# First attention's scores: two 128-row products per component replaced by three 64-row products, the two components side by side in the array's rows

## The chip, the cores and the metric

The kernel runs on one core of a Trainium2 chip. The metric is device time in microseconds (us) of one execution; less is better. Five engines work side by side on a core, each through its own queue in order: PE (TensorE, matrix products), DVE (VectorE), ACT (ScalarE), POOL (GpSimd) and SP (SyncE, which here only issues DMA transfers). A matrix product takes a stationary operand, which is loaded into PE's array first (rows "PEld" of the profile), and a moving operand that streams past it; the contraction runs over the partitions, and the result lands in a bank of PSUM, the accumulator memory, from where DVE or ACT must read it before the bank can be used again.

## The reference, cut to what matters

One decoder layer on a sequence of 1024 positions with model width 1024. Its first attention is a differential attention: 4 heads, each with two components of width 64, whose two softmaxes are subtracted. The other parts (a dilated window attention, gates, output projections, a gated feed-forward layer with a short convolution) are not touched by the change.

```python
def diff_attention(q, k, v, lam):        # q, k: (B, S, H, 2, 64), v: (B, S, H, 128)
    scale = dqk ** -0.5
    def one_block(args):                 # one block of 128 queries
        qi, i = args
        sc = jnp.einsum('bqhcd,bkhcd->bchqk', qi, k).astype(jnp.float32) * scale
        qpos = i * Q_BLOCK + jnp.arange(Q_BLOCK)
        causal = kpos[None, :] <= qpos[:, None]
        p = jax.nn.softmax(jnp.where(causal, sc, -jnp.inf), axis=-1)
        a = p[:, 0] - lam * p[:, 1]
        return jnp.einsum('bhqk,bkhd->bqhd', a, v)
```

Before this, q and k of a head are projections of the normed input, turned by rotary embedding. All of it is asked for in float32.

## The kernel before

**Precision.** PE works here on operands of a type called fp32r, and the kernel does not take one fp32r copy of a float32 operand as exact enough. So an operand is split into a high part (a copy to fp32r, done by ACT) and a low part (operand minus high part, done by DVE); the helper is `split`, whose two instructions show as L149 (ACT) and L146 (DVE). A product of two split operands is three PE products, high by high, low by high and high by low; the helper is `mm3`, lines L155, L156 and L157.

**Projection.** `proj_t` loads the weights of 128 columns, and for each half of the sequence (512 positions) makes 8 times `mm3` into one PSUM bank (the tile `acc`), 24 products of 512 columns. When the bank is full, an evacuation function is called. For the first attention, `proj_a(h)` does this for q and then for k of head h. The 128 rows of the result are the head's two components, 64 rows each. The evacuation first calls `rotated`: four ACT copies (L684) and three DVE instructions (L685 to L687), which leave the turned half in a tile `t`.

**How q and k are laid out.** The scores of one component have a contraction of 64, half of the array's rows. The kernel uses the other half for the low part. For component 0, tile `q0` holds the high part of q in rows 0 to 63 and its low part in rows 64 to 127; `k0` holds the high part of k in both halves of the rows, and `l0` the low part of k in both. Then q0 by k0 is high by high plus low by high, and q0 by l0 is high by low plus low by low. So a component takes two 128-row products, L765 and L766. (`q1`, `k1` and `l1` are the same for component 1.) This layout costs 64-row instructions: for a half of q two ACT copies (L730, L731) and two DVE subtractions (L732, L733), for a half of k four ACT copies (L738, L739, two each) and four DVE subtractions (L742). Every head takes six tiles from a ring of 18 (`slot`).

**Scores.** `attend_a(h, i)` handles one block of 128 queries, i from 0 to 7. It needs the scores against the first (i+1)*128 keys, cut into pieces of at most 512 columns: one piece for i up to 3, two for i from 4 to 7. For each component, and for each of its pieces, it takes a PSUM bank from a pool of two (tile `s` on PE, `ps_s` in the code), makes the two products, and has DVE add the mask, find the row's maximum and write the scores to SBUF (L768). Then ACT takes the exponential (L777), DVE combines the two components (L784), and the block's probabilities are later turned on PE (L697) and multiplied with v (L710, L713).

**Order of the work.** The program is written as one stream, and a scheduler at build time orders it for each engine: of the instructions whose operands and buffers it expects to be there, it takes the one that stands first in the stream, with the attention's pieces moved ahead by 30 places (`high_priority(offset=30)`). The blocks of a head come in the order i = 6, 7, 4, 5, 2, 3, 0, 1. Between them stand other pieces of work that only need PE and its operands (`interleave`, `A_FILLS`): the projections of the next head, gates, and for the last head the first projections of the dilated attention. So the products of a projection stand between the products of the scores on PE wherever a score product was not expected to be ready.

Of the kernel before, what the change touches and what calls it, by code (L numbers as in the profile page):

```python
# [15 lines left out]
F32 = mybir.dt.float32  # L16
F32R = mybir.dt.float32r
I32 = mybir.dt.int32
AF = mybir.ActivationFunctionType
ALU = mybir.AluOpType  # L20
# [4 lines left out]
P = 128  # L25
S = 1024
# [33 lines left out]
QA, KA, VA, QB, KB, VB, GT = 0, 512, 1024, 1536, 3072, 4608, 6144  # L60
# [27 lines left out]
def trunk(ctx: ExitStack, tc: tile.TileContext, a, out):  # L88
    nc = tc.nc
# [17 lines left out]
    def psum(dt=F32, pool=acc, tag="acc"):  # L107
        return pool.tile([P, 512], dt, tag=tag, name=tag)
# [39 lines left out]
    def split(hi, lo, src, eng=None):  # L148
        copy = nc.scalar.activation(hi, src, AF.Copy)  # L149
        sub(eng or nc.vector, lo, src, hi)  # L150
        return copy.ins
# [83 lines left out]
    def proj_t(col, evacuate):  # L235

        wh, wl = load_unit(w_in[where[col]])
        for half, sl in enumerate(halves()):
            ps = psum()
            for k in range(KC):  # L240
                w = slice(k * P, (k + 1) * P)
                mm3(ps, wh[:, w], wl[:, w], xh[:, k, sl], xl[:, k, sl], k == 0, k == KC - 1)
                if k == KC - 1:
                    evacuate(half, sl, ps)
                if k % 2:
                    yield 0.5
# [65 lines left out]
    ps_s = open_pool(attn, "ps_s", bufs=2, space=PSUM)  # L312
# [18 lines left out]
    def slot(name, shape=(P, S), dt=F32R):  # L331

        return slots.tile(list(shape), dt, tag="slot", name=name, bufs=SLOTS)
# [111 lines left out]
    with ExitStack() as st_y:  # L445
# [115 lines left out]
        with ExitStack() as st0:  # L561
# [18 lines left out]
            for j in range(KC):  # L580
# [7 lines left out]
                c = 0  # L588
# [27 lines left out]
        for n in range(8, len(steps_v)):  # L616
# [25 lines left out]
            if k == 0 and (p, i) in places_y:  # L642
                q, name, pool = places_y[p, i]
# [12 lines left out]
    cos_a, sin_a = load_tabs(64, 32)  # L656
# [22 lines left out]
    def rotated(ps, cos, sin, sl, quarter):  # L679
        t1 = rt.tile([P, 512], F32, tag="t1", name="t1")  # L680
        t2 = rt.tile([P, 512], F32, tag="t2", name="t2")
        for q in range(P // quarter):
            src, dst = slice((q ^ 1) * quarter, ((q ^ 1) + 1) * quarter), slice(q * quarter, (q + 1) * quarter)
            nc.scalar.activation(t1[dst], ps[src], AF.Copy)  # L684
        nc.vector.tensor_tensor(t2, ps, cos[:, sl], op=ALU.mult)  # L685
        nc.vector.tensor_tensor(t1, t1, sin[:, sl], op=ALU.mult)
        nc.vector.tensor_tensor(t2, t2, t1, op=ALU.add)  # L687
        return t2
# [28 lines left out]
    wk_a = open_pool(st_a, "work_a", side="right")  # L717
# [4 lines left out]
    u, v = slice(0, 64), slice(64, 128)  # L722

    def proj_a(h, res):
        q0, q1, k0, k1, l0, l1 = (slot(n) for n in ("q0", "q1", "k0", "k1", "l0", "l1"))
        res += [q0, q1, k0, k1, l0, l1]

        def put_q(half, sl, ps):
            t = rotated(ps, cos_a, sin_a, sl, 32)
            nc.scalar.activation(q0[u, sl], t[u], AF.Copy)  # L730
            nc.scalar.activation(q1[v, sl], t[v], AF.Copy)  # L731
            nc.vector.tensor_tensor(q0[v, sl], t[u], q0[u, sl].bitcast(F32), op=ALU.subtract)  # L732
            nc.vector.tensor_tensor(q1[u, sl], t[v], q1[v, sl].bitcast(F32), op=ALU.subtract)  # L733

        def put_k(half, sl, ps):
            t = rotated(ps, cos_a, sin_a, sl, 32)
            for part, kk in ((u, k0), (v, k1)):
                nc.scalar.activation(kk[u, sl], t[part], AF.Copy)  # L738
                nc.scalar.activation(kk[v, sl], t[part], AF.Copy)  # L739
            for part, kk, ll in ((u, k0, l0), (v, k1, l1)):  # L740
                for to in (u, v):
                    nc.vector.tensor_tensor(ll[to, sl], t[part], kk[part, sl].bitcast(F32), op=ALU.subtract)  # L742

        yield from proj_t(QA + h * P, put_q)
        yield from proj_t(KA + h * P, put_k)

    def attend_a(h, i, ops, vs, out_sb, pair):

        q0, q1, k0, k1, l0, l1 = ops
        scale = QK ** -0.5  # L750
        if i // 4 not in out_sb:
            out_sb[i // 4] = (wk_a.tile([P, 512], F32, tag="osb", name="osb", bufs=2),
                              tiny.tile([P, 4], F32, tag="eps4", name="eps4", bufs=2))
        osb, eps4 = out_sb[i // 4]
        qs = slice(i * P, (i + 1) * P)
        w = (i + 1) * P
        chunks = [(c, min(w, c + 512)) for c in range(0, w, 512)]
        mx = tiny.tile([P, 2, 2], F32, tag="mx", name="mx")
        sc = []
        for c, (qq, kk, ll) in enumerate(((q0, k0, l0), (q1, k1, l1))):  # L760
            s_sb = wk_a.tile([P, S], F32, tag="s", name="s", bufs=4)
            sc.append(s_sb)
            for n, (c0, c1) in enumerate(chunks):
                ps = psum(F32, ps_s, "s")[:, : c1 - c0]
                nc.tensor.matmul(ps, qq[:, qs], kk[:, c0:c1], start=True, stop=False)  # L765
                nc.tensor.matmul(ps, qq[:, qs], ll[:, c0:c1], start=False, stop=True)  # L766
                mask = mask_a[:, 512 - (c1 - c0) :] if c1 == w else mask_a[:, 0:1].to_broadcast([P, 512])
                nc.vector.tensor_tensor_reduce(  # L768
                    out=s_sb[:, c0:c1], in0=ps, in1=mask, scale=1.0, scalar=-3.0e38,
                    op0=ALU.add, op1=ALU.max, accum_out=mx[:, c, n : n + 1])  # L770
        if len(chunks) == 2:
            nc.vector.tensor_tensor(mx[:, :, 0], mx[:, :, 0], mx[:, :, 1], op=ALU.max)
        negm = tiny.tile([P, 2], F32, tag="negm", name="negm")
        nc.vector.tensor_scalar(negm, mx[:, :, 0], -scale, None, op0=ALU.mult)
        den = tiny.tile([P, 2], F32, tag="den", name="den")
        for c in range(2):
            exp = nc.scalar.activation(sc[c][:, :w], sc[c][:, :w], AF.Exp, bias=negm[:, c : c + 1], scale=scale,  # L777
                                       accum_out=den[:, c : c + 1])
        marks["ACT"] = exp.ins
        rc = tiny.tile([P, 1], F32, tag="rc", name="rc")  # L780
        nc.vector.reciprocal(rc, den[:, 1:2])
        ratio = tiny.tile([P, 1], F32, tag="ratio", name="ratio")
        nc.vector.scalar_tensor_tensor(ratio, rc, den[:, 0:1], nlam, op0=ALU.mult, op1=ALU.mult)
        nc.vector.scalar_tensor_tensor(sc[0][:, :w], sc[1][:, :w], ratio, sc[0][:, :w], op0=ALU.mult, op1=ALU.add)  # L784

        nc.vector.scalar_tensor_tensor(eps4[:, i % 4 : i % 4 + 1], den[:, 0:1], EPS, den[:, 0:1], op0=ALU.mult, op1=ALU.mult)

        pair.append(sc[0])
        if i % 2 == 0:
            return  # L790
        two, po, ts = list(pair), [], {}
        pair.clear()
        groups = [[(b, n) for b in (2 * g, 2 * g + 1) for n in range(2) if b < i or n] for g in range((i + 1) // 2)]

        def turn(g):
            t = turned([two[n][:, b * P : (b + 1) * P] for b, n in groups[g]], wk_a, 3)
            for b in {b for b, _ in groups[g]}:
                at = [x for x, (bb, _) in enumerate(groups[g]) if bb == b]
                ts[b] = t[:, :, at[0] : at[-1] + 1]

        def add(b):
            if b == 0:
                po.append(psum(F32, ps_o, "o")[:, : 2 * P].rearrange("p (n q) -> p n q", n=2))
            uses = [(b, 0, 1, ts[b])] + ([(i, 1, 1, ts[i])] if b == i - 1 else [])
            pv(po[0], vs, uses, h % 2, b == 0, b == i - 1)
            if b == i - 1:
                o = osb[:, (i % 4 - 1) * P : (i % 4 + 1) * P].rearrange("p (n q) -> p n q", n=2)
                nc.scalar.activation(o, po[0], AF.Copy)
                if i % 4 == 1:
                    head_norm(h, i // 4, osb, eps4)  # L810

        def do(*todo):
            def fn():
                for f, x in todo:
                    f(x)
            return fn

        n = len(groups)
        later(1, do(*[(turn, g) for g in range(min(n, 2))]))
        if n > 2:  # L820
            later(1, do((turn, 2)))
            later(1, do((add, 0)))
        if n > 3:
            later(1, do((add, 1), (turn, 3)))
        for b in range({1: 0, 2: 0, 3: 1, 4: 2}[n], i):
            later(2, do((add, b)))
# [655 lines left out]
    def put(step, *srcs):  # L1482

        operands[step] = []
        for src in srcs:
            operands[step].append(next(places)())
            split(*operands[step][-1], src)
# [259 lines left out]
```

## Time and profile before

| what | value |
|---|---|
| median of 3 runs | 1698.27 us (1698.05 to 1699.11) |
| profiled execution, first to last instruction (span) | 1697.2 us |
| PE busy | 1683.2 us, 8076 products |
| DVE busy | 1344.4 us |
| ACT busy | 888.9 us |
| granted PE clock, mean | 0.999 |

The profiled execution's own time is known only by its span; it is 1.07 us below the median of the three runs, which is what lies around the first and last instruction and the spread between runs together.

How to read the rows. A row of groups names line, engine, operation, tiles (out<-in), shapes, count, then the busy time in us and the mean of one in ns. PE's recorded durations overlap from one product to the next, since products are pipelined, so what one costs is read from the distance of the starts in the timeline, not from its duration. A row of the timeline is start in us, duration in us, engine, line, operation, tiles. A row of windows gives the window, its length, and each engine's busy time with its count of instructions.

### The profile page before, as it was taken

To read this page: it belongs to the slowest core of one execution; us is meant where nothing else is said; L and a number is where in the kernel's file an instruction comes from. 1 tells how busy PE (TensorE), PEld (TensorE's weight loads), DVE (VectorE), ACT (ScalarE), POOL (GpSimd) and SP (SyncE) were. 2 spreads that over 40 slices of the span, in tenths; PEclk is the share of its full clock that TensorE was granted. 3 is DMA by queue.
4 is the path that set the end of the run, shared out by engine and by line. 5 is a ranking of instruction groups with operands and counts; after the bars stand their busy time and mean duration, and the time that the engine had idled before them with its cause. 6 is when DMAs were issued, how large, how long until landed. Compare 5 with 4: busy or idle time off the path is not lost.

```text
span 1697.2 us, 23030 instructions
## 1 busy us (share of the span) xinstructions
PE 1683.2 (99%) x8076; PEld 1410.1 (83%) x8076; DVE 1344.4 (79%) x2557; ACT 888.9 (52%) x1631; POOL 110.0 (6%) x174
## 2 busy tenths in 40 slices
PE   9999999999999999999999999999999999999997
PEld 7888888888888888888888888888888888888886
DVE  8795686877777776678756865899999989799967
ACT  7643575655544776667653533464344444355453
POOL 0031000000000000000123400300000000000000
PEclk9999999999999999999999999999999999999999
DMA  8767311214112213233675532132222222296524
GB/s 269 231 233 258 99 57 62 88 57 119 50 63 81 69 57 108 82 115 117 208 264 197 198 112 75 38 106 87 99 81 75 93 87 88 84 349 216 194 75 161
DMA packets 104451, 216.41 MB, mean 128 GB/s; under 512 B 12992, under 2 KB 22144, under 8 KB 104336
## 3 DMA queue, kind: packets, MB, share of 16 engines
q1 hardware_dynamic: 89296, 171.28, 30.6%
q0 software_dynamic: 10288, 35.28, 6.2%
q10 hardware_dynamic: 4752, 8.39, 1.3%
q8 instruction: 63, 1.03, 0.3%
q14 instruction: 52, 0.43, 0.1%
HBM read 167.05 MB, written 47.86 MB: 127 GB/s over the span
## 4 chain that ended last, share of the span: by engine, by line
PE 94%; DMA 3%; ACT 1%; DVE 1%; issue 1%; POOL 0%; SPq 0%; DVEq 0%; POOLq 0%
PE acc L155 21%; PE acc L157 21%; PE acc L156 21%; PE acc L1583 3%; PE acc L1581 3%; PE acc L1582 3%; PE o L710 2%; PE pt L697 2%; PE acc L1262 2%; PE acc L1260 2%; PE acc L1261 2%; PE o L713 1%; PE s L156 1%; PE s L157 1%; PE s L155 1%; PE s L766 1%
## 5 line engine op out<-in xcount | busy, mean ns | idle before, releaser
L155 PE MATMUL acc<-xh,whi 128*128 128x512 f32 x768 | 304.2, 396 | 0.0
L157 PE MATMUL acc<-xl,whi 128*128 128x512 f32 x768 | 303.8, 396 | 0.0
L156 PE MATMUL acc<-xh,wlo 128*128 128x512 f32 x768 | 303.1, 395 | 0.0
L149 ACT ACTIVATE whi<-raw 128x512 fp32r<-128x512 f32 (+1 forms) x252 | 156.0, 626 | 184.9 <-PE acc L157 98.4
L146 DVE TENSOR_TENSOR wlo<-raw,whi 128x512 fp32r<-128x512 f32 (+1 forms) x252 | 178.0, 713 | 39.4 <-ACT whi L149 36.7
L157 PEld LDWEIGHTS acc<-xl,whi 128*128 128x128 f32 x768 | 144.4, 188 | 27.7
L156 PEld LDWEIGHTS acc<-xh,wlo 128*128 128x128 f32 x768 | 144.4, 188 | 27.6
L155 PEld LDWEIGHTS acc<-xh,whi 128*128 128x128 f32 x768 | 144.5, 188 | 27.5 <-DVE t L685 0.2
L155 PE MATMUL acc<-mh,whi 128*128 128x512 f32 x400 | 155.8, 390 | 0.3 <-ACT mh L149 0.3
L156 PE MATMUL acc<-mh,wlo 128*128 128x512 f32 x400 | 155.6, 389 | 0.0
L157 PE MATMUL acc<-ml,whi 128*128 128x512 f32 x400 | 155.3, 389 | 0.0
L684 ACT ACTIVATE t<-acc 64x512 f32<-64x512 f32 (+1 forms) x160 | 94.7, 592 | 58.6 <-PE acc L157 56.7
L1458 DVE TENSOR_TENSOR u<-acc,u 128x512 f32<-128x512 f32 x133 | 90.8, 687 | 20.8 <-PE acc L157 20.7
L149 ACT ACTIVATE whi<-s 128x512 fp32r<-128x512 f32 x76 | 46.9, 627 | 102.1 <-PE acc L157 86.9
L685 DVE TENSOR_TENSOR t<-acc,cos 128x512 f32<-128x512 f32 x64 | 44.2, 691 | 58.9 <-ACT t L684 58.3
L155 PEld LDWEIGHTS acc<-mh,whi 128*128 128x128 f32 x400 | 75.1, 188 | 16.0 <-ACT mh L149 0.5
L157 PEld LDWEIGHTS acc<-ml,whi 128*128 128x128 f32 x400 | 75.1, 188 | 15.6
L156 PEld LDWEIGHTS acc<-mh,wlo 128*128 128x128 f32 x400 | 75.1, 188 | 15.5
L1582 PE MATMUL acc<-whi,wlo 128*128 128x512 f32 x220 | 77.5, 389 | 0.0
L1581 PE MATMUL acc<-whi 128*128 128x512 f32 x220 | 76.3, 389 | 0.0
L1583 PE MATMUL acc<-wlo,whi 128*128 128x512 f32 x220 | 73.2, 390 | 0.0
L768 DVE CUSTOM_DVE_ANT_0 s<-s,mask_a 128x512 f32<-128x512 f32 (+3 forms) x96 | 52.0, 553 | 23.2 <-PE s L766 14.6
(389 smaller groups left out, 3950.5 us busy)
## 6 DMA issues: line engine op xcount, KB each, us to landing
raw<-in_w_in SPq DMA_DIRECT2D x96, 256.0 KB, 2.9
raw<-in_w_up SPq DMA_DIRECT2D x88, 256.0 KB, 2.8
raw<-in_w_v SPq DMA_DIRECT2D x71, 256.0 KB, 4.6
raw<-c_d SPq DMA_DIRECT2D x48, 256.0 KB, 3.7
c_d<-c SPq DMA_DIRECT2D x22, 512.0 KB, 2.7
raw<-in_w_down SPq DMA_DIRECT2D x37, 256.0 KB, 4.4
v_d<-yv POOLq DMA_DIRECT2D x32, 256.0 KB, 4.8
gt_d<-gate ACTq DMA_DIRECT2D x32, 256.0 KB, 2.2
```

The source lines that it names most:

```text
L146: eng.tensor_tensor(lo, src, hi.bitcast(F32), op=ALU.subtract)
L149: copy = nc.scalar.activation(hi, src, AF.Copy)
L155: nc.tensor.matmul(o, sh, mh, start=first, stop=False, skip_group_check=on)
L156: nc.tensor.matmul(o, sl, mh, start=False, stop=False, skip_group_check=on)
L157: nc.tensor.matmul(o, sh, ml, start=False, stop=last, skip_group_check=on)
L684: nc.scalar.activation(t1[dst], ps[src], AF.Copy)
L685: nc.vector.tensor_tensor(t2, ps, cos[:, sl], op=ALU.mult)
L768: nc.vector.tensor_tensor_reduce(out=s_sb[:, c0:c1], in0=ps, in1=mask, scale=1.0, scalar=-3.0e38, op0=ALU.add, op1=ALU.max, accum_out=mx[: ...
L1458: nc.vector.tensor_tensor(to, made(p), x, op=ALU.add)
L1581: nc.tensor.matmul(banks[m], gh[:, tk], wh, start=f == 0, stop=False)
L1582: nc.tensor.matmul(banks[m], gl[:, tk], wh, start=False, stop=False)
L1583: nc.tensor.matmul(banks[m], gh[:, tk], wl, start=False, stop=f == NH - 1)
```

## The change

The q and k of a head are split once, as everywhere else: a high tile and a low tile of 128 rows each, in which rows 0 to 63 are component 0 and rows 64 to 127 are component 1. A head takes four tiles from the ring. For each piece of columns `attend_a` takes both PSUM banks at once, and makes six products with 64 rows each: high by high for component 0 and then 1, low by high for 0 and 1, high by low for 0 and 1. The products of component 0 use rows 0 to 63 of the array, those of component 1 rows 64 to 127, each into its own bank. Then DVE evacuates the two banks. The product low by low, which came along before, is no longer made.

```diff
     def proj_a(h, res):
-        q0, q1, k0, k1, l0, l1 = (slot(n) for n in ("q0", "q1", "k0", "k1", "l0", "l1"))
-        res += [q0, q1, k0, k1, l0, l1]
-
-        def put_q(half, sl, ps):
-            t = rotated(ps, cos_a, sin_a, sl, 32)
-            nc.scalar.activation(q0[u, sl], t[u], AF.Copy)
-            nc.scalar.activation(q1[v, sl], t[v], AF.Copy)
-            nc.vector.tensor_tensor(q0[v, sl], t[u], q0[u, sl].bitcast(F32), op=ALU.subtract)
-            nc.vector.tensor_tensor(q1[u, sl], t[v], q1[v, sl].bitcast(F32), op=ALU.subtract)
-
-        def put_k(half, sl, ps):
-            t = rotated(ps, cos_a, sin_a, sl, 32)
-            for part, kk in ((u, k0), (v, k1)):
-                nc.scalar.activation(kk[u, sl], t[part], AF.Copy)
-                nc.scalar.activation(kk[v, sl], t[part], AF.Copy)
-            for part, kk, ll in ((u, k0, l0), (v, k1, l1)):
-                for to in (u, v):
-                    nc.vector.tensor_tensor(ll[to, sl], t[part], kk[part, sl].bitcast(F32), op=ALU.subtract)
-
-        yield from proj_t(QA + h * P, put_q)
-        yield from proj_t(KA + h * P, put_k)
+        qh, ql, kh, kl = (slot(n) for n in ("qh", "ql", "kh", "kl"))
+        res += [qh, ql, kh, kl]
+
+        def put(hi, lo):
+            def evacuate(half, sl, ps):
+                split(hi[:, sl], lo[:, sl], rotated(ps, cos_a, sin_a, sl, 32))
+            return evacuate
+
+        yield from proj_t(QA + h * P, put(qh, ql))
+        yield from proj_t(KA + h * P, put(kh, kl))
...
-        sc = []
-        for c, (qq, kk, ll) in enumerate(((q0, k0, l0), (q1, k1, l1))):
-            s_sb = wk_a.tile([P, S], F32, tag="s", name="s", bufs=4)
-            sc.append(s_sb)
-            for n, (c0, c1) in enumerate(chunks):
-                ps = psum(F32, ps_s, "s")[:, : c1 - c0]
-                nc.tensor.matmul(ps, qq[:, qs], kk[:, c0:c1], start=True, stop=False)
-                nc.tensor.matmul(ps, qq[:, qs], ll[:, c0:c1], start=False, stop=True)
-                mask = mask_a[:, 512 - (c1 - c0) :] if c1 == w else mask_a[:, 0:1].to_broadcast([P, 512])
+        sc = [wk_a.tile([P, S], F32, tag="s", name="s", bufs=4) for _ in range(2)]
+        for n, (c0, c1) in enumerate(chunks):
+            pss = [psum(F32, ps_s, "s")[:, : c1 - c0] for _ in range(2)]
+            for x, (qq, kk) in enumerate(((qh, kh), (ql, kh), (qh, kl))):
+                for ps, rows in zip(pss, (u, v)):
+                    nc.tensor.matmul(ps, qq[rows, qs], kk[rows, c0:c1], start=x == 0, stop=x == 2)
+            mask = mask_a[:, 512 - (c1 - c0) :] if c1 == w else mask_a[:, 0:1].to_broadcast([P, 512])
+            for c, ps in enumerate(pss):
                 nc.vector.tensor_tensor_reduce(
-                    out=s_sb[:, c0:c1], in0=ps, in1=mask, scale=1.0, scalar=-3.0e38,
+                    out=sc[c][:, c0:c1], in0=ps, in1=mask, scale=1.0, scalar=-3.0e38,
                     op0=ALU.add, op1=ALU.max, accum_out=mx[:, c, n : n + 1])
```

More of the change, by code (lines that the diff above doesn't have):

```diff
@@ L724, in proj_a @@
     def proj_a(h, res):
-        q0, q1, k0, k1, l0, l1 = (slot(n) for n in ("q0", "q1", "k0", "k1", "l0", "l1"))
-        res += [q0, q1, k0, k1, l0, l1]
-        def put_q(half, sl, ps):
-            t = rotated(ps, cos_a, sin_a, sl, 32)
-            nc.scalar.activation(q0[u, sl], t[u], AF.Copy)
-            nc.scalar.activation(q1[v, sl], t[v], AF.Copy)
-            nc.vector.tensor_tensor(q0[v, sl], t[u], q0[u, sl].bitcast(F32), op=ALU.subtract)
-            nc.vector.tensor_tensor(q1[u, sl], t[v], q1[v, sl].bitcast(F32), op=ALU.subtract)
-        def put_k(half, sl, ps):
-            t = rotated(ps, cos_a, sin_a, sl, 32)
-            for part, kk in ((u, k0), (v, k1)):
-                nc.scalar.activation(kk[u, sl], t[part], AF.Copy)
-                nc.scalar.activation(kk[v, sl], t[part], AF.Copy)
-            for part, kk, ll in ((u, k0, l0), (v, k1, l1)):
-                for to in (u, v):
-                    nc.vector.tensor_tensor(ll[to, sl], t[part], kk[part, sl].bitcast(F32), op=ALU.subtract)
-        yield from proj_t(QA + h * P, put_q)
-        yield from proj_t(KA + h * P, put_k)
+        qh, ql, kh, kl = (slot(n) for n in ("qh", "ql", "kh", "kl"))
[6 more added lines that the diff above has]
+        yield from proj_t(KA + h * P, put(kh, kl))
     def attend_a(h, i, ops, vs, out_sb, pair):
-        q0, q1, k0, k1, l0, l1 = ops
+        qh, ql, kh, kl = ops
         scale = QK ** -0.5
```

## The prediction, made before the changed kernel was run

> **What bounds the kernel now.** I read the page first, then the windows of the stage that the change touches, then the chain of waits there.
>
> ```profile
> span 1697.2 us, 23030 instructions
> PE 1683.2 (99%) x8076; PEld 1410.1 (83%) x8076; DVE 1344.4 (79%) x2557; ACT 888.9 (52%) x1631; POOL 110.0 (6%) x174
> ```
> ```profile
> core 0: us, PE busy (x) PEld busy (x) DVE busy (x) ACT busy (x) POOL busy (x), PEclk, DMA share, GB/s
> 175.00:505.00 330.00, 330.00 (x1702) 280.70 (x1702) 249.74 (x667) 186.27 (x357) 0.00 (x0) 1.00 0.23 74
> ```
> ```profile
> by line: PE acc L155 24.2%; PE acc L156 24.2%; PE acc L157 24.2%; PE s L766 5.7%; PE s L765 5.7%; PE o L710 5.4%; PE pt L697 5.1%; PE o L713 3.1%; PE o L839 1.5%; PE pt L847 0.9%
> ```
>
> PE is busy for 99% of the span. From 175 to 505 us, where the first attention runs, it is busy for 330.00 of 330.00 us at full clock, while DVE and ACT have 80 and 144 us to spare. The chain from 200 to 506 us holds PE alone, and the score products L765 and L766 have 11.4% of it, 34.9 us. So in this stage time is the room that products take on PE, and nothing else: a product added or removed lengthens or shortens the kernel by its spacing, and work removed from DVE or ACT does nothing by itself.
>
> **What the splits are worth.**
>
> ```profile
> L742 DVE TENSOR_TENSOR l<-t,k 64x512 fp32r<-64x512 f32 x32 | 21.9, 685 | 0.5
> L687 DVE TENSOR_TENSOR t<-t,t 128x512 f32<-128x512 f32 x64 | 43.9, 686 | 0.4
> ```
> ```profile
> L738 ACT ACTIVATE k<-t 64x512 fp32r<-64x512 f32 x16 | 10.1, 628 | 3.7 <-DVE t L687 3.5
> ```
>
> A DVE instruction on 64 rows takes as long as one on 128 (685 and 686 ns). For each half of a head's sequence the layout takes 2 + 4 copies on ACT and 2 + 4 subtractions on DVE, and the new one takes 1 + 1 on each; with 8 halves over the four heads that is 32 fewer on each, 32 x 0.685 = 21.9 us of DVE and 32 x 0.628 = 20.1 us of ACT. All of it lies beside a PE that never idles in this stage, so I cost it at nothing. Two ring tiles fewer per head are nothing for the same reason.
>
> **What a score product costs now.**
>
> ```profile
> L766 PE MATMUL s<-l,q 128*128 128x512 f32 x48 | 18.8, 391 | 0.0
> L766 PE MATMUL s<-l,q 128*128 128x384 f32 x16 | 5.4, 339 | 0.0
> L766 PE MATMUL s<-l,q 128*128 128x256 f32 x16 | 4.5, 281 | 0.0
> L766 PE MATMUL s<-l,q 128*128 128x128 f32 x16 | 4.4, 276 | 0.0
> ```
> ```profile
> 289.08 0.40 PE L765 MATMUL s<-k,q 128*128 128x512 f32 x1
> 289.31 0.40 PE L766 MATMUL s<-l,q 128*128 128x512 f32 x1
> 289.54 0.34 PE L765 MATMUL s<-k,q 128*128 128x384 f32 x1
> 289.72 0.34 PE L766 MATMUL s<-l,q 128*128 128x384 f32 x1
> 289.90 0.40 PE L155 MATMUL acc<-xh,whi 128*128 128x512 f32 x1
> ```
> ```profile
> 312.06 0.22 PE L765 MATMUL s<-k,q 128*128 128x128 f32 x1
> 312.12 0.28 PE L766 MATMUL s<-l,q 128*128 128x128 f32 x1
> 312.23 0.45 PE L156 MATMUL acc<-xh,wlo 128*128 128x512 f32 x1
> ```
> ```profile
> 326.92 0.28 PE L765 MATMUL s<-k,q 128*128 128x256 f32 x1
> 327.04 0.28 PE L766 MATMUL s<-l,q 128*128 128x256 f32 x1
> 327.15 0.40 PE L157 MATMUL acc<-xl,whi 128*128 128x512 f32 x1
> ```
> ```profile
> 282.28 0.95 PE L839 MATMUL o<-ones,sq 128*128 128x1 f32 x8
> 283.08 0.49 PE L765 MATMUL s<-k,q 128*128 128x512 f32 x1
> ```
>
> The distance from start to start is 0.23 us at 512 columns, 0.18 at 384, 0.115 at 256, and 0.06 and 0.11 (mean 0.085) at 128. There are 96, 32, 32 and 32 of them (L765 has the counts of L766): 22.1 + 5.8 + 3.7 + 2.7 = 34.3 us, as the chain says. The counts make 48 pairs (one piece of columns, both components), of four products each: 24 pairs of 512 columns, and 8 of each narrower width. I call the room of one product a slot. The eight L839 take 0.80 us though they stream a single column each: 0.10 us per product is a floor under narrow ones, which goes by the weights that each one loads.
>
> **What a pair costs after.** Six products of 64 rows instead of four of 128. If two neighbours, one per half of the array, run at once, a pair that stays in the order 0,1,0,1,0,1 takes 3 slots; with no overlap it takes 6. No product of this trace uses half of the rows, so these are the two ends. I take the overlap as happening where two such products are neighbours (other rows, other bank, and two loads of 0.10 us fit under a slot of 0.23), but not below the floor: two overlapping products need 0.20 us at any width. The other end is a rival. The Trainium skill ("TensorE: Matmul & The Clock Gate", Part 3) says that products in different row groups run concurrently and gives 3.07 times for four of 32 rows; an estimate by that figure is 6 / (2 x 0.77) = 3.9 slots for a pair in the best order, no gain over 4. No row here tests it.
>
> **In which order they come** decides the sum, and the buffers decide the order.
>
> ```profile
> 295.22 0.69 DVE L768 CUSTOM_DVE_ANT_0 s<-s,mask_a 128x512 f32<-128x512 f32 x1 [1.20 <-PE s L766]
> 297.27 0.68 DVE L768 CUSTOM_DVE_ANT_0 s<-s,mask_a 128x512 f32<-128x512 f32 x1
> 302.25 0.69 DVE L768 CUSTOM_DVE_ANT_0 s<-s,mask_a 128x512 f32<-128x512 f32 x1
> 302.86 0.69 DVE L768 CUSTOM_DVE_ANT_0 s<-s,mask_a 128x512 f32<-128x512 f32 x1
> ```
> ```profile
> 299.61 0.40 PE L765 MATMUL s<-k,q 128*128 128x512 f32 x1
> 301.67 0.39 PE L765 MATMUL s<-k,q 128*128 128x512 f32 x1
> ```
> ```profile
> L768 DVE CUSTOM_DVE_ANT_0 s<-s,mask_a 128x512 f32<-128x512 f32 x48 | 32.9, 688 | 18.9 <-PE s L766 11.1 <-PE pt L697 7.3
> L768 DVE CUSTOM_DVE_ANT_0 s<-s,mask_a 128x384 f32<-128x384 f32 x16 | 8.8, 552 | 1.4 <-PE s L766 1.0
> L768 DVE CUSTOM_DVE_ANT_0 s<-s,mask_a 128x256 f32<-128x256 f32 x16 | 6.6, 419 | 0.4 <-PE pt L697 0.2
> L768 DVE CUSTOM_DVE_ANT_0 s<-s,mask_a 128x128 f32<-128x128 f32 x16 | 4.6, 285 | 2.5 <-PE s L766 2.5
> ```
>
> Two evacuations start 2.05 us apart, and the products that take the freed banks start 2.06 us apart, 4.4 us later each. So the scheduler puts a score product where it expects its bank to be free, and projections in between; PE itself doesn't wait. After the change both banks of a pair are full at nearly the same time, and DVE empties them one after the other. Back to back, the second starts 0.61 us after the first at 512 columns (302.25, 302.86), and by the means of the rows (each less about 0.08) 0.47, 0.34 and 0.21 at 384, 256 and 128. That is how much later bank 1 comes free than bank 0. Component 0's next product is ready in that time and stands ahead of the projection, so the scheduler takes all of component 0's that fit before component 1 may start:
> - lag under one slot of the new pair: 0,1,0,1,0,1, 3 slots;
> - under two: 0,0,1,1,0,1, 4 slots with two neighbourings;
> - under three: 0,0,0,1,1,1, 5 slots with one;
> - more: a projection product between the threes, no neighbours, 6 slots.
>
> A head's pieces, each with the width before it in brackets, and what it then costs over today's four slots, in us: 512 (256) 0; 384 (512) six slots, +0.36; 512 (384) five, +0.23; 512 (512) +0.23; 512 (512) +0.23; 128 (512) six at the floor, 0.60 for 0.34, +0.26; 512 (128) three, -0.23; 256 (512) six, +0.23; 384 (256) four, two of them at the floor, +0.04; 512 (384) +0.23; 128 (512) +0.26; 256 (128) four, two at the floor, +0.17. The sum is 2.01 us a head, **+8.0 us** for four.
>
> **Going in and out of 64 rows.**
>
> ```profile
> 613.20 0.40 PE L155 MATMUL acc<-xh,whi 128*128 128x512 f32 x1
> 613.44 0.60 PE L1038 MATMUL pt<-ident,stat 128*4 128x128 f32 x4
> 613.79 0.47 PE L156 MATMUL acc<-xh,wlo 128*128 128x512 f32 x1
> 614.11 0.39 PE L157 MATMUL acc<-xl,whi 128*128 128x512 f32 x1
> ```
>
> Each time full products meet half ones the array is used another way: twice for a pair in one piece, four times for one with a projection between, 8 x 2 + 4 x 4 = 32 a head, 128 in all. The lower end of the price is nothing: the nearest rows, four products with 4 columns of weights instead of 128 between two full ones, take 0.35 us and put the next start no later than four of the floor's 0.10 would. The upper end is the overlap of neighbours, lost: recorded 0.39 us against a spacing of 0.23, so 0.16. The rows at hand stand near the lower end, but they use all rows; I take a fifth, 0.03, **+3.8 us** (0 to 20.5). The Trainium skill ("TensorEngine Tiling (Array Packing)", Key Properties) says that a change of tiling mode, unlike a change of tile, drains TensorE; no row here shows it, and it is the third rival's mechanism.
>
> The sum is +11.8 us. The span of 1697.2 us becomes 1709.0; the span lies 1.07 us below the median of the runs, 1698.27, so the forecast is **1710.1 us**.
>
> **The rivals.**
> 1. *No overlap.* Six slots everywhere: 24 x 0.46 + 8 x 0.36 + 8 x 0.23 + 8 x 0.26 = +17.8, with the 3.8 of the switches +21.6: 1719.9. For it: PE in this trace never shows two products streaming at once. Against: they use other rows and banks. Chance 0.22.
> 2. *Pairs stay together, and the time falls.* If the scheduler reaches the score products late, because other products stand ahead of them, both banks are free and the order is 0,1,0,1,0,1. Three slots, loads side by side too: a quarter of 34.3, -8.6, or 1689.7 with free switches; with the floor in force -0.23 x 24 - 0.12 x 8 + 0.14 x 8 + 0.26 x 8 = -3.3. It decides where the lag of bank 1 stays under one slot, 0.23 us. The pair at 289.08, where two banks are taken without a projection between, speaks for it; the 2.06 us at 299.61 against. Chance of a gain over 0.2%: 0.17.
> 3. *Each switch costs the whole overlap.* 8.0 + 128 x 0.16 = +28.5: 1726.8. Chance 0.12.
> 4. *Nothing to measure.* Half of the pairs stay together, or all with the floor in force: within 3.4 us of now. Chance 0.17.
> That the change would not do what it says (the two halves of q and k not landing in other rows) is rival 1 in its effect.
>
> **How the numbers follow.** A measurement can tell 0.2%, 3.4 us, from no change. The forecast has 0.32, rivals 1 and 3 have 0.22 and 0.12, so slower has 0.66; rival 4 gives same 0.17, rival 2 faster 0.17. The range goes from 1691, which holds rival 4 and the smaller gains of rival 2, to 1728, just over rival 3; left out are the full gain and rival 3 without overlap, together less than 2 in 10. The likeliest case's own range, with the switches from 0 to 0.06 us, is 1706 to 1714.
>
> **What would show it.** The changed profile's timeline of PE from 200 to 500 us should show score products of one component in a row, then the other's, mostly broken by projections; neighbours of the two components should start almost together, or 0.23 us apart if rival 1 holds. The first full product after a pair shows the switch: about 0.26 us after the last score product, or 0.39 for rival 3. PE's busy share in the stage should stay full, DVE fall by some 22 us and ACT by 20. The prediction is wrong if the chain's share of the score products falls, or if PE shows idle time in front of them, a wait for DVE that I have at nothing.

## The result, and the profile after

The changed kernel takes 1747.52 us (median of 4 runs, 1745.94 to 1749.09) against 1698.69 us: a ratio of 1.029, 95% interval 1.0277 to 1.0302. It is 48.8 us slower. The forecast was 11.8 us slower, and the range ended at 1728.

The page's head, with PE's row of the first part, of the changed kernel:

```profile
span 1747.3 us, 23165 instructions
PE 1730.7 (99%) x8172; PEld 1415.2 (81%) x8172; DVE 1326.7 (76%) x2525; ACT 869.4 (50%) x1599; POOL 109.2 (6%) x174
```

The stage by windows, first of the kernel before, then of the changed one (the window's length, then PE, PEld, DVE, ACT and POOL, each with its count, then the granted clock, the DMA share and GB/s), and the changed kernel's chain of waits from 200 to 540 us, by line:

```profile
175.00:560.00 385.00, 385.00 (x1981) 327.32 (x1981) 289.29 (x769) 215.48 (x414) 1.14 (x4) 1.00 0.23 73
```
```profile
175.00:560.00 385.00, 385.00 (x1852) 292.66 (x1851) 238.65 (x662) 172.63 (x337) 1.32 (x4) 1.00 0.19 64
```
```profile
by line: PE acc L155 22.1%; PE acc L157 22.1%; PE acc L156 21.8%; PE s L753 18.5%; PE o L710 5.4%; PE pt L697 4.8%; PE o L713 2.8%; PE o L827 1.6%; PE pt L835 0.9%
```

DVE lost 17.7 us and ACT 19.5, and the kernel got nothing for it. PE is busy for all of 385 us, as it was: no wait took the place of a wait. The score products (now L753) hold 18.5% of 340 us in the chain, 62.9 us, where they held 34.9; so 28 of the 49 us are in their own rows. The other 20 stand beside them, in rows where nothing was changed. The timeline of PE around one run of three score products shows it:

```profile
282.00 0.39 PE L156 MATMUL acc<-xh,wlo 128*128 128x512 f32 x1
282.23 0.39 PE L157 MATMUL acc<-xl,whi 128*128 128x512 f32 x1
282.55 0.49 PE L753 MATMUL s<-kh,qh 64*128 64x512 f32 x1
282.88 0.39 PE L753 MATMUL s<-kh,ql 64*128 64x512 f32 x1
283.12 0.39 PE L753 MATMUL s<-kl,qh 64*128 64x512 f32 x1
283.44 0.50 PE L155 MATMUL acc<-xh,whi 128*128 128x512 f32 x1
283.77 0.40 PE L156 MATMUL acc<-xh,wlo 128*128 128x512 f32 x1
```

All products here have 512 columns, and ordinary ones start 0.23 us apart. Going in, 0.32 us pass to the first 64-row product and 0.33 to the second; then 0.24; going out again 0.32 and 0.33. From 282.23 to 283.77 there are five products in 1.54 us, where five at the usual spacing (0.227 us, to one digit more) take 1.13: the two ends of the run cost **0.41 us, 0.20 per end**. The rows of weight loads (PEld) in the same stretch say what an end is made of:

```profile
282.00 0.19 PEld L157 LDWEIGHTS acc<-xl,whi 128*128 128x128 f32 x1
282.54 0.18 PEld L753 LDWEIGHTS s<-kh,qh 64*128 64x128 f32 x1 [0.35 <-DVE rhw L175]
282.65 0.19 PEld L753 LDWEIGHTS s<-kh,ql 64*128 64x128 f32 x1
282.88 0.18 PEld L753 LDWEIGHTS s<-kl,qh 64*128 64x128 f32 x1
283.44 0.19 PEld L155 LDWEIGHTS acc<-xh,whi 128*128 128x128 f32 x1 [0.37 <-issue]
283.55 0.19 PEld L156 LDWEIGHTS acc<-xh,wlo 128*128 128x128 f32 x1
```

Usually a product's weights are loaded while the product before it streams: L157's load starts at 282.00, a whole slot ahead of its product at 282.23. At an end, the load starts with its own product (282.54 and 282.55; 283.44 and 283.44), and both some 0.09 us late. So an end is about 0.09 us in which nothing is issued, and then 0.11 us of a weight load that nothing hides. The instruction that the profile puts down as the releaser at 282.54 (DVE L175, which ran from 282.26 to 282.42) is not the reason: going out, and at the next run shown, the profile names no releaser ("issue"), and the delay is the same.

One run in which the pair stayed together, six products of 256 columns, again from PE's timeline:

```profile
333.41 0.39 PE L156 MATMUL acc<-xh,wlo 128*128 128x512 f32 x1
333.73 0.39 PE L753 MATMUL s<-kh,qh 64*128 64x256 f32 x2
333.95 0.29 PE L753 MATMUL s<-kh,ql 64*128 64x256 f32 x2
334.06 0.29 PE L753 MATMUL s<-kl,qh 64*128 64x256 f32 x2
334.28 0.39 PE L710 MATMUL o<-pt,vh 128*128 128x256 f32 x1
334.50 0.28 PE L713 MATMUL o<-pt,vl 128*128 128x256 f32 x1
```

Each row is two products ("x2"), one per component, that start within about 0.01 us of each other. Six of them take the room of three, and in the middle of the run a pair takes 0.11 us: the overlap is whole, weight loads included, whose rows are pairs too:

```profile
333.72 0.19 PEld L753 LDWEIGHTS s<-kh,qh 64*128 64x128 f32 x2 [0.36 <-issue]
333.83 0.20 PEld L753 LDWEIGHTS s<-kh,ql 64*128 64x128 f32 x2
333.95 0.20 PEld L753 LDWEIGHTS s<-kl,qh 64*128 64x128 f32 x2
```

**The account.** Of the products in the order of the trace, those of the scores form 95 runs: 62 of three (61 of them the three products of one component), 10 of six, 23 broken otherwise. Take, for every run, the time from the start of the product before it to the start of the second product after it, less the ordinary slots of these two neighbours. The sum is 84.5 us; for the 84 runs of the kernel before it is 36.3. The difference, 48.2 us, is all but 1.9 of the span's 50.1. And 95 x 0.41 = 39.0 us of it are ends; what is left, 45.5 us of slots, is 9.2 over the kernel before. This split can be checked from the order itself: counting each product at the spacing of its width, and two that start together once, the slots come to 44.5 us and the ends to 0.42 us a run; for the runs of three, the median is 0.40 to 0.43 at each of the four widths.

Outside this sum lies one stretch in which PE is busy at a lower clock: from 310.8 to 314.2 us its granted clock is 0.51, and projection products with 128 rows start about 0.43 us apart instead of 0.23, which costs about 1.6 us. What lowered the clock there is not shown.

### The profile page after: what moved, and what is told of

The parts are those of the page before. It is cut to its first block, busy times and chain, and to the rows that moved or that the text cites. A ratio compares the mean times of both kernels' runs of the same rounds, so it can differ in the third digit from the quotient of the medians.

```text
span 1747.3 us, 23165 instructions
## 1 busy us (share of the span) xinstructions
PE 1730.7 (99%) x8172; PEld 1415.2 (81%) x8172; DVE 1326.7 (76%) x2525; ACT 869.4 (50%) x1599; POOL 109.2 (6%) x174
## 4 chain that ended last, share of the span: by engine, by line
PE 96%; DMA 3%; ACT 1%; issue 0%; DVE 0%; SPq 0%; POOL 0%; DVEq 0%; POOLq 0%; ACTq 0%
PE acc L155 21%; PE acc L157 21%; PE acc L156 21%; PE s L753 4%; PE acc L1570 3%; PE acc L1571 3%; PE acc L1569 3%; PE o L710 2%; PE pt L697 2%; PE acc L1248 2%; PE acc L1249 2%; PE acc L1250 2%; PE o L713 1%; PE s L156 1%; PE s L157 1%; PE s L155 1%
## 5 line engine op out<-in xcount | busy, mean ns | idle before, releaser
L155 PE MATMUL acc<-xh,whi 128*128 128x512 f32 x768 | 308.0, 401 | 0.0
L157 PE MATMUL acc<-xl,whi 128*128 128x512 f32 x768 | 307.2, 400 | 0.0
L157 PEld LDWEIGHTS acc<-xl,whi 128*128 128x128 f32 x768 | 144.9, 189 | 34.5 <-issue 6.4
L157 PE MATMUL acc<-ml,whi 128*128 128x512 f32 x400 | 155.3, 389 | 0.0
L157 PEld LDWEIGHTS acc<-ml,whi 128*128 128x128 f32 x400 | 75.1, 188 | 15.5
```

Source lines behind the costliest of these rows:

```text
L155: nc.tensor.matmul(o, sh, mh, start=first, stop=False, skip_group_check=on)
L157: nc.tensor.matmul(o, sh, ml, start=False, stop=last, skip_group_check=on)
```

## The experiments

The theories, as the expectations name them. **A:** each run of 64-row products costs 0.41 us at its ends, whatever its length, and neighbours of the two components overlap. **B:** the ends are free, and 64-row products just take more room when they do not overlap. **C:** time is lost because both banks are taken at once. Below, "room" is the sum described in the account above.

### e1_pairs_kept: 48 runs of six

```diff
-            pss = [psum(F32, ps_s, "s")[:, : c1 - c0] for _ in range(2)]
-            for x, (qq, kk) in enumerate(((qh, kh), (ql, kh), (qh, kl))):
-                for ps, rows in zip(pss, (u, v)):
-                    nc.tensor.matmul(...)
+            both = ps_a.tile([P, 1024], F32, tag="s", name="s")   # ps_a: one buffer of two banks; the opening of the pools is left out here
+            pss = [both[:, x : x + c1 - c0] for x in (0, 512)]
+            with tc.high_priority(offset=100):
+                for x, (qq, kk) in enumerate(((qh, kh), (ql, kh), (qh, kl))):
+                    for ps, rows in zip(pss, (u, v)):
+                        nc.tensor.matmul(...)
```

Expected:

> The two banks of a pair are one tile of two banks, so they come free together, and the six products stand 100 places further ahead: in the order that is built there are 48 runs of six 64-row products, where the changed kernel has 95 runs. Theory A (each run of 64-row products costs 0.41 us at its two ends, whatever its length, and neighbours of the two components overlap): 48 x 0.41 + three slots a pair, 25.7, is 45.4 us against 34.3 to 36.3 before, so 1707 to 1711. Theory B (the ends are free, 64-row products just take more room when they don't overlap): only the slots change, some 20 us off 1747.5, 1727. Theory C (time is lost because both banks are taken at once): no better than 1747, as the banks now come free even later.

Measured: 1715.19 us (1712.26 to 1718.58), ratio 1.0096 (1.0081 to 1.0112). PE's timeline around one run:

```profile
309.43 0.39 PE L155 MATMUL acc<-xh,whi 128*128 128x512 f32 x1
309.75 0.50 PE L758 MATMUL s<-kh,qh 64*128 64x512 f32 x2
310.09 0.40 PE L758 MATMUL s<-kh,ql 64*128 64x512 f32 x2
310.32 0.40 PE L758 MATMUL s<-kl,qh 64*128 64x512 f32 x2
310.65 0.50 PE L156 MATMUL acc<-xh,wlo 128*128 128x512 f32 x1
310.99 0.40 PE L157 MATMUL acc<-xl,whi 128*128 128x512 f32 x1
```

The spacings are those of the run of three (0.32, 0.34, 0.23, 0.33, 0.34), with twice the products. Two thirds of the loss are gone with half of the runs. The time is 4 us above A's range, 12 us below B's 1727 and 32 below C's 1747, so it is nearest to A. The room is 44.6 us, 8.3 over the kernel before, where A had 9 to 11; the profiled execution's span is 13.2 us longer, so some 5 us are lost elsewhere: from 560 to 640 us PE is busy for 78.59 of 80 us at a granted clock of 0.98, about 3 us of them (see e2).

### e3_full_rows: the same six products on all rows

```diff
-            for x, (qq, kk) in enumerate(((qh, kh), (ql, kh), (qh, kl))):
-                for ps, rows in zip(pss, (u, v)):
-                    nc.tensor.matmul(ps, qq[rows, qs], kk[rows, c0:c1], start=x == 0, stop=x == 2)
+            for x, (qq, kk) in enumerate((((h0, h1), kh), ((l0, l1), kh), ((h0, h1), kl))):
+                for ps, q in zip(pss, qq):    # h0, l0 are zero in rows 64-127; h1, l1 in rows 0-63
+                    nc.tensor.matmul(ps, q[:, qs], kk[:, c0:c1], start=x == 0, stop=x == 2)
```

> The same six products a pair in the same order over two banks, but with 128 rows each: the high and low tiles of q are kept once per component with zeros in the other component's 64 rows. Nothing can overlap and nothing changes the array's use. Theory A: six slots for four, +17.8 us on before: 1714 to 1719, some 30 us faster than the changed kernel. Theory B: as the products cannot overlap at all, no faster than the changed kernel, 1747 or more. Theory C: as the changed kernel, 1747.

Measured: 1717.2 us (1716.57 to 1719.48), ratio 1.011 (1.0095 to 1.0125); room 54.0 us, 17.7 over before, where six slots for four were to give 17.8. Six products in sequence, with half of the array multiplying by zero, are 30 us faster than the same six with 64 rows each. B falls with this, and C too as the main cause, since this kernel takes both banks at once like the changed one.

### e4_half_extra and e5_full_extra: the price of an end by itself

Both are the kernel before with one more product in each of its 96 groups, in the same order on PE. They differ in rows alone:

```diff
-                nc.tensor.matmul(ps, qq[:, qs], ll[:, c0:c1], start=False, stop=True)
+                nc.tensor.matmul(ps, qq[:, qs], ll[:, c0:c1], start=False, stop=False)
+                nc.tensor.matmul(ps[:, :P], qq[u, qs], kk[u, c0 : c0 + P], start=False, stop=True)   # e5: [:, ...]
```

> The kernel before with one more product in each of the 96 groups of a component's piece, 128 columns wide, on rows 0 to 63 (high by high is added once more for these columns, so the scores differ). 96 of them, each alone between 128-row products. Theory A: 96 x 0.41 = 39 us on top of the same kernel with 128-row extra products, 1746 to 1750. Theory B: the same as with 128-row extra products, 1707 to 1710. Theory C: likewise.

> The same as the kernel with an extra product on rows 0 to 63 but on all 128 rows (q's tile by k's, once more for these columns, so the scores differ); the order of PE's products is the same. All theories: 96 products of 128 columns at 0.085 to 0.11 us each, +8 to +11: 1707 to 1710.

Measured: 1742.78 us with 64 rows (1741.86 to 1743.49), 1712.86 with 128 (1710.6 to 1713.95). 96 small products that multiply half as much cost 29.9 us more. The 128-row ones add 10.9 us of room (47.2 for 36.3), as expected; the time is some 3 us above the expected range, and the one with 64 rows 3 us below A's. PE's timeline with 64 rows, then with 128:

```profile
294.41 0.40 PE L766 MATMUL s<-l,q 128*128 128x512 f32 x1
294.74 0.33 PE L767 MATMUL s<-k,q 64*128 64x128 f32 x1
294.99 0.44 PE L765 MATMUL s<-k,q 128*128 128x384 f32 x1
295.27 0.34 PE L766 MATMUL s<-l,q 128*128 128x384 f32 x1
```
```profile
291.46 0.39 PE L766 MATMUL s<-l,q 128*128 128x512 f32 x1
291.69 0.22 PE L767 MATMUL s<-k,q 128*128 128x128 f32 x1
291.75 0.45 PE L765 MATMUL s<-k,q 128*128 128x512 f32 x1
292.03 0.40 PE L766 MATMUL s<-l,q 128*128 128x512 f32 x1
```

The 64-row product holds PE for 0.33 us before, 0.25 at, and 0.28 after it, where the slots would be 0.23, 0.06 and 0.18: 0.39 us too much, the two ends again. The 128-row one delays its follower by 0.05 us (0.28 for 0.23): its own 0.06 and these 0.05 are 0.11 us, what an open load of weights took above, so a product of 128 columns seems too short to cover one. That is why the difference is 31.9 us of room (79.0 and 47.2), 0.33 per product, and not 39. Theory A stands; its number for this pair was 9 us too high because it left out what a narrow product of 128 rows pays itself.

### e2_both_banks: the order without the 64-row products

```diff
-        for c, (qq, kk, ll) in enumerate(((q0, k0, l0), (q1, k1, l1))):
...
+        for n, (c0, c1) in enumerate(chunks):
+            pss = [psum(F32, ps_s, "s")[:, : c1 - c0] for _ in range(2)]
+            for x, ops_x in enumerate((((q0, k0), (q1, k1)), ((q0, l0), (q1, l1)))):
+                for ps, (qq, kk) in zip(pss, ops_x):
+                    nc.tensor.matmul(ps, qq[:, qs], kk[:, c0:c1], start=x == 0, stop=x == 1)
```

> The kernel before with its own layout and its own two 128-row products per component, but in the changed kernel's order: both banks of a pair taken at once, component 0 and 1 in turn, and the two evacuations behind one another. Theory A (the loss is what each run of 64-row products costs at its ends): nothing changes on PE, 1696 to 1702. Theory C (time is lost because both banks are taken at once): most of the loss is here, 1730 or more.

Measured: 1712.22 us (1709.44 to 1713.96), ratio 1.0077 (1.0062 to 1.0092). This is a miss for A, which had no change, though far from C's 1730. The score products are not where it went: their room is 38.0 us, 1.7 over before. The windows of this kernel, in the columns of the stage's rows above, and PE's waits from 490 to 640 us, say where most of it is:

```profile
175.00:560.00 385.00, 384.22 (x1955) 325.49 (x1954) 283.71 (x732) 210.61 (x400) 2.14 (x4) 1.00 0.21 72
560.00:640.00 80.00, 75.12 (x428) 63.82 (x428) 56.77 (x156) 56.02 (x132) 0.00 (x0) 0.96 0.18 64
```
```profile
PE pt L697 <- ACT bs L982: 2.1, 5, 1.4
PE s L155 <- DVE bmx L974: 1.3, 1, 1.3
PE o L710 <- ACT osb L1010: 0.8, 2, 0.6
PE s L155 <- ACT kh L876: 0.3, 1, 0.3
```

At the start of the dilated attention, in which the score products of the first have ended, PE idles 4.9 of 80 us and its granted clock falls to 0.96, which is worth another 3.2; the kernel before is busy for 79.97 of them at 1.00. That is 8 of the 12 us by which the span grew beyond the room; the other 4 are open. The scheduler built another order there; what in it makes PE wait was not followed further. The changed kernel has none of this: from 560 to 880 us its PE is busy for 320.00 of 320.00 us. So taking both banks at once can cost nearly 14 us by the order that follows from it, but this is not part of the 48.8.

### e6_half_mid128 and e7_half_mid32: what an end is made of

The kernel before with a 64-row product between the two of each group; its weights have 128 columns in the one and 32 in the other.

```diff
+                nc.tensor.matmul(ps[:32, :P], qq[u, i * P : i * P + 32], kk[u, c0 : c0 + P], start=False, stop=False)   # e6: 128
                 nc.tensor.matmul(ps, qq[:, qs], ll[:, c0:c1], start=False, stop=True)
```

> The kernel before with one product more on rows 0 to 63, 128 columns wide, between the two 128-row products of each of the 96 groups (the scores differ). Its pair with the next kernel: as e4_half_extra, 1739 to 1747.

> The same, but the extra product's weights have 32 columns instead of 128 (only the first 32 queries of a block are touched), so that its weights load sooner. If the end of a run costs a wait of 0.09 us and then a load of weights of 0.11 us that nothing hides, the entry becomes cheaper by about 0.08 us: 96 x 0.08 = 8 us under e6_half_mid128. If an end has one fixed price, whatever is loaded, both take the same time.

Measured: 1741.17 us (1740.82 to 1742.64) and 1734.47 (1732.34 to 1736.23): 6.7 us less, where 8 were expected, and 7.9 us less room (79.5 and 71.6), 0.082 per product. The two are not in the same order on PE (the score products form 87 runs and 80), but the time at the extra product itself does not hang on that: over all 96 its median is 0.254 and 0.174 us, 7.7 us in all. PE's timeline, 128 columns of weights first:

```profile
297.52 0.40 PE L765 MATMUL s<-k,q 128*128 128x512 f32 x1
297.85 0.33 PE L766 MATMUL s<-k,q 64*128 64x128 f32 x1
298.10 0.50 PE L767 MATMUL s<-l,q 128*128 128x512 f32 x1
298.44 0.34 PE L765 MATMUL s<-k,q 128*128 128x384 f32 x1
```
```profile
292.43 0.40 PE L765 MATMUL s<-k,q 128*128 128x512 f32 x1
292.75 0.25 PE L766 MATMUL s<-k,q 64*32 64x128 f32 x1
292.93 0.50 PE L767 MATMUL s<-l,q 128*128 128x512 f32 x1
293.27 0.34 PE L765 MATMUL s<-k,q 128*128 128x384 f32 x1
```

Only the time at the 64-row product changes, from 0.25 to 0.18 us; the 0.33 before it and the 0.34 after the next stay. An end is a wait that does not change with what is loaded, and a load of weights that lies open. (The product with 32 columns of weights also uses fewer of the array's columns; this was not tested apart.)

### e8_tile_only and e9_priority_only: how many runs, and why

e8 is e1 without the priority, e9 the changed kernel with that priority alone.

> As e1_pairs_kept, one tile of two banks for a pair, but without moving the six products further ahead: 66 runs of 64-row products in the order that is built, 33 of them of six. Theory A (0.41 us a run, overlap between neighbours): 66 x 0.41 = 27 and about 30 of slots, +20.6 on before, 1717 to 1724. Theory C (time is lost because both banks are taken at once): the same two banks as in e1_pairs_kept, so the same time as that, 1712 to 1718.

> The changed kernel with its two separate banks, the six products moved 100 places further ahead: 89 runs in the order that is built, 69 of them of three. If the banks' coming free one after the other splits the pairs, and not the place in the stream, little changes: theory A gives 89 x 0.41 = 36.5 and about 45 of slots, +45 on before, 1740 to 1748. If the place in the stream was what split them: near e1_pairs_kept, 1715.

Measured: 1726.9 us for e8 (1726.27 to 1728.08), 1746.4 for e9 (1745.86 to 1747.0). The kernels with the changed one's six 64-row products, in order of their runs: 48 runs 1715.2 us, 66 runs 1726.9, 89 runs 1746.4, 95 runs 1747.5. Their room over before is 8.3, 18.4, 46.8 and 48.2 us. e9 shows that the place in the stream does not split the pairs: with two banks that come free one after the other, 69 of 89 runs are threes, and the time lies within A's 1740 to 1748. e8's room is what A had (18.4 for 20.6), but its span grew by 27.9 us, so 9.5 us were lost elsewhere and the time lies above the expectation; PE is busy for 315.40 of the 320 us from 560 to 880 us, where the kernel before has 319.36; it is the same place as in e2.

## Why the prediction was wrong

- *PE is the bound, work taken off DVE and ACT gives nothing:* right. 17.7 and 19.5 us went (21.9 and 20.1 were expected), and PE stayed busy throughout the stage.
- *No new wait of PE for DVE:* right in the changed kernel; its stage has no idle time.
- *Neighbours of the two components overlap:* right, and rival 1 fell: they start within about 0.01 us. The Trainium skill ("TensorE: Matmul & The Clock Gate", Part 3) says so too; but the factor of 3.07 for four that the page gives, which as an estimate would have left a pair at 3.9 slots, has no counterpart here, where six products take three slots.
- *A floor of 0.20 us under two overlapping products:* wrong. Their weight loads run side by side, two products of 256 columns in 0.11 us. It was a small term.
- *The banks come free one after the other and split the pairs:* right. 61 of the 95 runs are the three products of one component, and the slots cost 9.2 us more than before, where the prediction had 8.0. That the banks are the cause is shown by e9 and e1: with the same place in the stream, two separate banks give 69 runs of three, and one tile of two banks gives 48 runs of six.
- *Each change between 64 and 128 rows costs 0.03 us, 128 times:* **this step failed.** It costs 0.20 us, 190 times: 39 us in place of 3.8. The count was too low because a projection came between the two threes of most pairs (62 runs of three and 10 of six, where it had 32 and 32), and because 23 runs broken otherwise were not foreseen; the price was taken near its lower end because products with 4 columns of weights, the nearest rows, cost nothing extra. They keep all 128 rows, and what costs is the change of rows. The upper end was too low as well: 0.16 us counted only the overlap of neighbours that a drain would lose, not the load of weights that then has nothing to hide under. So the range, which ended just over rival 3, could not hold the time.
- Rival 3 came nearest: its price sits on each change, as measured, with 0.16 us in place of 0.20 and 128 changes in place of 190. The Trainium skill's sentence ("TensorEngine Tiling (Array Packing)", Key Properties) that a change of tiling mode drains TensorE, and a change of tile does not, is borne out here on both sides: 0.20 us from 128 rows to 64 and as much back, while products on the upper and the lower rows start at most 0.02 us apart. The prediction gave it a chance of 0.12 on the strength of rows that did not test it.

## What to carry to other kernels

Two half-row products next to each other do run as one, weight loads and all, but the way into 64 rows and back costs 0.41 us, as much as 1.8 products of 512 columns: count the runs in the order that is built, not the products. A pair of 512 columns that stays together takes three slots instead of four and so saves 0.23 us. By this estimate, which no run tests, every run would need two such pairs (four banks) only to break even; with two banks the best order that was tried, 48 runs, is still 1.0% slower than the layout that fills the other half of the rows with the low parts. And where a price has no row in the trace and a stated rule speaks against the low end, measure it, or take the whole of it.

## What the runs showed that was not expected

- A change between 128-row and 64-row products costs about 0.09 us in which nothing is issued and 0.11 us of an open weight load (0.03 us for weights of 32 columns instead of 128, by the 0.08 us that e7 saves), going in and coming out, and whatever the width of the products: a run of three and a run of six cost the same.
- Weight loads for the two halves of the rows go side by side: in e1 and in the changed kernel each pair of loads stands as one row "x2", and six products take no longer than three of one component.
- Six 128-row products in sequence with zeros in half of their rows (1717.2 us) are as good as the best order that was tried of six overlapping 64-row ones (1715.2 us) here.
